# Padding a recurrence's matmuls to the full array, pairing the value products of attention and re-measuring the placing costs, in a hybrid decoder trunk

## The chip, the cores and the metric

The kernel runs on one core of a Trainium2 chip. The metric is the device time of one execution in microseconds (us).

## The reference

One layer with a residual, on x of 512 tokens by 2048 channels, all in float32:

```python
h = _rms(x, norm_g[l])
proj = h @ w_in[l]                       # 57 column tiles of 128
r, k, v, ga, wd, ad = _split(pa, ...)    # 12 RWKV heads of 64, after a token shift
def step(state, inp):
    sa = einsum('bhvk,bhk->bhv', state, -kk_t)
    state = state * w_t + sa[..., None] * (kk_t * a_t) + v_t[..., None] * k_t
    return state, einsum('bhvk,bhk->bhv', state, r_t)
...
z = einsum('bhqd,bhkd->bhqk', q, k)      # 12 stick-breaking attention heads, blocks of 128
w = where(causal, exp(log_sigmoid(z) + after), 0.0)
o = einsum('bhqk,bhkd->bhqd', w, v)
...
y = concatenate([ya, yb, yc], axis=-1) @ w_out[l]
x = x + y
```

Branch B is a trailing mean over 2 to 16 tokens and a small matmul. Each branch is gated by a SiLU of a part of the projection, and the RWKV output goes through a group norm first.

## The kernel before

TensorE (PE) computes the projection one column tile at a time (`project`): 16 blocks of the contraction, and for each the three products of a split into a high and a low part (`three`), so 48 matmuls of 128 x 512 named `pj` a tile, in the rounded type float32r. Six pairs of heads follow each other: four RWKV tiles, four attention tiles each; then eight tiles of the pooling branch. At the end the output projection (`oacc`) takes four column blocks of 512, each 192 matmuls over the 16 branch tiles.

Everything else is written as generators (`rwkv(p)`, `attention(p)`, `pooling(g)`), and `pump` resumes them between the `pj` matmuls. A generator yields a function made by `need` that says from when its next step may be placed. That time comes from `Pace`, a table of costs that counts the PE's matmuls as a clock and books work of VectorE (DVE), ScalarE (ACT) and GpSimd (POOL). So the order of PE's instructions is fixed when the program is built, and each engine executes its own instructions in that order. `high_priority` moves an instruction ahead on its engine.

For a pair of heads, `rwkv(p)` builds decay factors, then per chunk of 64 tokens the coupling matrices (`gm`, L588). The triangular inverse of 32 x 32 blocks is made on DVE, after a trip through DRAM (`s1`, `s2`), in 30 dependent steps of two instructions on `xblk` and `pr` (L620 to 626); two sets of 16 small products (`q1`, `q2`) put the blocks of an inverse together in `lt`. Then eight chunks follow each other serially (L687 to 717): product `w` and its copy `wsb`; product `u` with the inverse and its copies into `uv`; product `s` that updates the state, `se` and `uv`; and two products that add up the output `y`. Every one of these is issued once for each head, on 64 rows or 64 columns of the array. After the last chunk come the group norm (products `mu` and `var`) and the gate. `rwkv(p+1)` starts when `done[("mid", p)]` is set, just before the chunks of pair p.

`attention(p)` computes the scores `z` of a head in four products of 128 rows and four of 64 rows (the correction with `klo`, L778), and the value products `o` of one head at a time on 64 columns (L831). Where a float32 matmul (not float32r) is issued, the trace shows it as two instructions on PE; they are called passes.

All tiles are done before the output projection: `while len(tasks) > 1: pump(True)` (L940), which places what is left without asking `need`.

Of the kernel before, what the change touches and what calls it, by code (L numbers as in the profile page):

```python
# [8 lines left out]
F32 = mybir.dt.float32  # L9
# [43 lines left out]
BANKS = {"pj": 2, "g": 3, "c": 3}  # L53
# [3 lines left out]
EVACUATE = 25  # L57
DL = 4.0
# [28 lines left out]
Y_TILE = {("a", i): i for i in range(6)} | {("b", i): 6 + i for i in range(4)} | {("c", i): 10 + i for i in range(6)}  # L87


class Pace:  # L90
# [37 lines left out]
    def cost(self, eng, f, out, ins):  # L128
        n = self.free(out)
        if eng == "act":  # L130
            return 0.2 + n * 0.00083
        if eng == "pool":
            if f in ("memset", "affine_select"):
                return 0.05 + n * 0.0011
            return 0.08 + n * (0.0028 if f == "tensor_scalar" else 0.0033)
# [16 lines left out]
    def matmul(self, out, lhsT, rhs):  # L152
        n = self.free(rhs)
        m = self.free(lhsT)
        if rhs.dtype == F32R:
            c = max(n / 2400.0, m * 0.00083)
        else:
            c = max(4 * max(n, 64) / 2400.0, 0.1) * (0.6 if m <= 64 or rhs.shape[0] <= 64 else 1.0)
# [45 lines left out]
def hybrid_trunk_kernel(ctx: ExitStack, tc: tile.TileContext, x, xT, w_in, w_out, vecs, consts, up_w, pool_w, out, tap=None):  # L204
# [15 lines left out]
    tp = ctx.enter_context(tc.tile_pool(name="tp", bufs=14))  # L220
# [57 lines left out]

    hh = [hp.tile([P, T], F32R, tag=f"hh{k}", name=f"hh{k}") for k in range(KT)]
# [14 lines left out]
    for pl, tag, parts in ((ap, "q2", 1), (ap, "k2", 1), (ap, "w3", 1), (rp, "bk", 2), (rp, "bkt", 2), (rp, "rx", 2),  # L294
                           (rp, "uv", 2), (rp, "amr", 3), (ap, "wt", 2)):
        xt = pl.tile([P, parts, T], F32, tag=tag, name=name("x"))
# [208 lines left out]

    def rwkv(p):
# [13 lines left out]
        mm(dec, upl[lo, 0:P], wd2[lo, :], False, True)  # L520
# [4 lines left out]
        mm(av, upl[hi, P:2 * P], ad2[hi, :], False, True)  # L525
# [35 lines left out]
        amr = rp.tile([P, NC_, 3, C], F32, tag="amr", name=name("amr"))  # L561
        for h, s in ((0, lo), (1, hi)):
# [7 lines left out]
        dve.tensor_tensor(amr[:, :, 2, :], r3, e[:, :, 1:], ALU.mult)  # L570
# [7 lines left out]
        lt = rp.tile([P, NC_, C], F32, tag="lt", name=name("lt"))  # L578
        ms = strict.rearrange("p (o t) -> p o t", o=1)
        mi = incl.rearrange("p (o t) -> p o t", o=1)  # L580
        for half in range(2):
            cs = slice(4 * half, 4 * half + 4)
            for h, s, other in quad:
                yield need(*([amr, bk] if half == 0 and h == 0 else []), tag="g")
# [6 lines left out]
                dve.tensor_tensor(lt[s, cs, :], g4[s, :, 0, :], ms[s].to_broadcast([HD, 4, C]), ALU.mult)  # L591
# [5 lines left out]
        s2v = s2.rearrange("(c h b) s t -> s c h b t", h=2, b=2)  # L597
        for h in range(2):
            for b in range(2):
                r0 = h * HD + b * B  # L600
                dma(out=s1v[:, :, h, b, :], in_=lt[r0:r0 + B, :, b * B:(b + 1) * B])
# [7 lines left out]


        nblk = rp.tile([P, B, B], F32, tag="bk", name=name("nblk"))
        xblk = tmp("xblk", 8 * B).rearrange("p (i t) -> p i t", t=B)
        s1r = s1.rearrange("k (i g) t -> g k i t", g=4)
        s2r = s2.rearrange("k (i g) t -> g k i t", g=4)
        for r in range(4):
            dma(out=nblk[r * B:(r + 1) * B], in_=s1)
        dma(out=xblk, in_=s1r)
        yield soon(xblk)
        pr = tmp("pr")
        for j in range(1, B - 1):  # L620
            m = B - 1 - j
            ni = (j + 3) // 4
            prv = pr[:, :ni * m].rearrange("p (s t) -> p s t", t=m)
            dve.tensor_tensor(prv, xblk[:, 0:ni, j:j + 1].to_broadcast([P, ni, m]),
# [427 lines left out]
```

## Time and profile before

| | |
|---|---|
| median of 3 runs | 1089.75 us (1088.41 to 1089.97) |
| the profiled execution | 1089.68 us; span from its first to its last instruction 1088.0 us |
| busy: PE, DVE, ACT, POOL | 98%, 68%, 39%, 13% of the span |
| mean granted clock of TensorE | 0.993 |
| first and last `pj`, first and last `oacc` (start) | 42.1 and 907.8, 908.0 and 1083.9 us |

A busy share counts overlapped, pipelined instructions; the distance from the start of one PE instruction to the start of the next is what each costs. An edge, in what follows, is the extra distance where a matmul on the whole array stands next to one on a part of it.

### The profile page before, as it was taken

To read this page: it belongs to the slowest core of one execution; us is meant where nothing else is said; L and a number is where in the kernel's file an instruction comes from. 1 tells how busy PE (TensorE), PEld (TensorE's weight loads), DVE (VectorE), ACT (ScalarE), POOL (GpSimd) and SP (SyncE) were. 2 spreads that over 40 slices of the span, in tenths; PEclk is the share of its full clock that TensorE was granted. 3 is DMA by queue.
4 is the path that set the end of the run, shared out by engine and by line. 5 is a ranking of instruction groups with operands and counts; after the bars stand their busy time and mean duration, and the time that the engine had idled before them with its cause. 6 is when DMAs were issued, how large, how long until landed. Compare 5 with 4: busy or idle time off the path is not lost.

```text
span 1088.0 us, 14731 instructions
## 1 busy us (share of the span) xinstructions
PE 1066.2 (98%) x5552; PEld 801.3 (74%) x5552; DVE 737.6 (68%) x1596; ACT 427.8 (39%) x670; POOL 143.1 (13%) x208
## 2 busy tenths in 40 slices
PE   9998999999999999999999999999999999999998
PEld 7877766687666877668766787667776677888887
DVE  6266978759787797778877799777986457223232
ACT  6453525235353354334543345524443235111111
POOL 0031113101132011210211102210021111000000
PEclk9999999999999999899999999999999999999999
DMA  9513231132211321113221132112221125444232
GB/s 329 204 63 105 80 93 40 56 92 84 84 48 51 107 85 66 58 59 97 86 76 39 64 115 77 61 58 84 100 78 55 48 94 163 149 154 137 96 137 75
DMA packets 58185, 101.92 MB, mean 94 GB/s; under 512 B 29312, under 2 KB 30720, under 8 KB 58112
## 3 DMA queue, kind: packets, MB, share of 16 engines
q1 hardware_dynamic: 58112, 100.96, 28.2%
q8 instruction: 44, 0.72, 0.3%
q14 instruction: 29, 0.24, 0.1%
HBM read 95.17 MB, written 5.77 MB: 93 GB/s over the span
## 4 chain that ended last, share of the span: by engine, by line
PE 80%; DVE 10%; issue 4%; ACT 2%; DMA 2%; POOL 2%; SPq 0%; POOLq 0%; DVEq 0%; ACTq 0%
PE pj L350 45%; PE oacc L350 15%; PE first L350 3%; PE o L350 2%; PE z L350 2%; DVE w L198 2%; DVE wl L198 2%; PE gm L350 2%; PE y L350 2%; PE w L350 2%; PE wT L354 1%; DVE xblk L198 1%; PE u L350 1%; POOL e L198 1%; PE s L350 1%
## 5 line engine op out<-in xcount | busy, mean ns | idle before, releaser
L350 PE MATMUL pj<-hl,wh 128*128 128x512 f32 x864 | 349.0, 404 | 0.0
L350 PE MATMUL pj<-hh,wh 128*128 128x512 f32 x864 | 347.9, 403 | 1.0 <-DVE u L198 0.8
L350 PE MATMUL pj<-hh,wl 128*128 128x512 f32 x864 | 347.6, 402 | 0.0
L198 DVE TENSOR_TENSOR wl<-raw,wh 128x1024 fp32r<-128x1024 f32 x140 | 172.1, 1229 | 168.6 <-ACT wh L198 162.8
L198 ACT CAST wh<-raw 128x1024 fp32r<-128x1024 f32 x140 | 147.0, 1050 | 312.7 <-PE pj L350 187.5
L350 PEld LDWEIGHTS pj<-hh,wh 128*128 128x128 f32 x864 | 163.1, 189 | 38.0 <-issue 4.4
L350 PEld LDWEIGHTS pj<-hh,wl 128*128 128x128 f32 x864 | 163.2, 189 | 35.4 <-issue 0.4
L350 PEld LDWEIGHTS pj<-hl,wh 128*128 128x128 f32 x864 | 163.1, 189 | 35.5 <-issue 1.2
L350 PE MATMUL oacc<-wl,yh 128*128 128x512 f32 x256 | 100.1, 391 | 0.8 <-DVE wl L198 0.8
L350 PE MATMUL oacc<-wh,yl 128*128 128x512 f32 x256 | 99.6, 389 | 0.0
L350 PE MATMUL oacc<-wh,yh 128*128 128x512 f32 x256 | 99.6, 389 | 0.0
L198 POOL TENSOR_SCALAR e<-e 128x512 f32<-128x512 f32 x28 | 49.0, 1749 | 327.9 <-ACT e L198 327.6
L198 POOL TENSOR_TENSOR d<-u 128x512 f32<-128x512 f32 x25 | 34.2, 1370 | 230.9 <-DVE u L198 148.6
L350 PEld LDWEIGHTS oacc<-wl,yh 128*128 128x128 f32 x256 | 48.0, 188 | 11.5 <-DVE wl L198 1.3
L350 PEld LDWEIGHTS oacc<-wh,yl 128*128 128x128 f32 x256 | 48.1, 188 | 10.0 <-issue 0.2
L350 PEld LDWEIGHTS oacc<-wh,yh 128*128 128x128 f32 x256 | 48.0, 188 | 10.0
L198 DVE TENSOR_TENSOR xblk<-xblk,pr 128x60 f32<-128x60 f32 (+8 forms) x180 | 44.5, 247 | 4.1
L198 ACT ACTIVATE e<-e 128x512 f32<-128x512 f32 x50 | 31.4, 629 | 39.1 <-POOL e L198 38.8
L198 DVE TENSOR_TENSOR_SCAN w<-kon,n 128x512 f32<-128x512 f32 (+3 forms) x48 | 39.3, 841 | 6.6 <-POOL n L198 6.5
L198 DVE TENSOR_TENSOR pr<-xblk,nblk 128x60 f32<-128x60 f32 (+8 forms) x180 | 38.7, 215 | 4.4
L198 DVE TENSOR_TENSOR u<-pj,rstd 128x512 f32<-128x512 f32 x50 | 34.3, 686 | 8.3 <-PE pj L350 7.9
L198 ACT ACTIVATE n<-n 128x512 f32<-128x512 f32 (+1 forms) x72 | 38.9, 557 | 1.3
(195 smaller groups left out, 1262.7 us busy)
## 6 DMA issues: line engine op xcount, KB each, us to landing
raw<-in_w_in SPq DMA_DIRECT2D x108, 512.0 KB, 3.4
raw<-in_w_out SPq DMA_DIRECT2D x32, 512.0 KB, 3.4
xs<-in_x SPq DMA_DIRECT2D x8, 512.0 KB, 4.7
xr<-in_x SPq DMA_DIRECT2D x16, 256.0 KB, 5.3
out<-xr SPq DMA_DIRECT2D x16, 256.0 KB, 3.2
fr<-in_w_in SPq DMA_DIRECT2D x12, 256.0 KB, 7.4
nblk<-s SPq DMA_DIRECT2D x24, 128.0 KB, 4.9
x<-in_xT SPq DMA_DIRECT2D x5, 512.0 KB, 7.4
```

The costliest lines, as they stand in the source:

```text
L198: return call(*args, **kw)
L350: pe.matmul(o, lhsT, rhs, start=start, stop=stop)
L354: pe.transpose(o, src, ident)
```

## The change

- **Full-size products.** `amr` and `lt` become lasting buffers whose unused halves are zero, so `w`, `u`, `s`, both `y` products and `gm` are single matmuls on 128 rows and 128 columns for both heads. `w`, `u` and `s` of a chunk share one PSUM bank (`wus`), and `y` of four chunks another. The low-order products of `dec`, `av` and `z` run over all 128 rows; `z` gets a zero-free copy `kl2` of the correction in both halves, made on POOL.
- **Paired value products.** `attention` handles both heads in one pass at the end: for each key block the product of head 0 and that of head 1 are issued one behind the other, on different columns of the array.
- **Placing costs.** `Pace.cost` and `Pace.matmul` get other numbers: a DVE instruction starts at 0.165 us instead of 0.065, a scan counts twice, copies on DVE are no longer halved, a matmul costs a little more.
- **The inverse** is a generator of its own, `inverse(p, s1, s2)`, spawned after `tr`; it yields after every third step instead of every sixth, and `rwkv(p)` waits for `done[("inv", p)]`.
- **Copies ahead.** The DVE copies between the products of a chunk are moved ahead by `SCAN` (40) places. `se` moves from DVE to POOL.
- **The end.** The branch tiles enter the output projection in `Y_ORDER`, with the last pair's (5 and 15) at the end, and nothing waits for all tasks any more: `split_y` places steps with `pump(True)` until the tile that it needs is done.
- The `tp` pool has 13 buffers instead of 14.

```diff
+SCAN = 40
+Y_ORDER = [0, 1, 2, 3, 4, 10, 11, 12, 13, 14, 6, 7, 8, 9, 5, 15]
...
-        if f in ("tensor_scalar", "tensor_copy", "memset") and not any(self.key(a) in self.read_psum for a in ins):
+        if f == "tensor_tensor_scan":
+            n *= 2
+        if f in ("tensor_scalar", "memset"):
             n *= 0.5
-        return 0.065 + n * 0.00104
+        return 0.165 + n * 0.00104
...
-            c = max(n / 2400.0, m * 0.00083)
+            c = max(n / 2400.0 + 0.010, 0.19 * m / 128)
...
+    def inverse(p, s1, s2):
...
+            if j % 3 == 0:
+                yield soon(xblk)
...
+        done[("inv", p)] = True
...
-                    rhs = amr[s, cc, 0:3:2, :] if h == 0 else amr[s, cc, 1:3, :]
-                    mm(g[:, j * P:(j + 1) * P], bk[s, cc, :, :], rhs)
+                    mm(g[:, j * P:(j + 1) * P], bk[:, cc, :, :], amr[:, cc, h:4:2, :])
...
+        spawn(inverse(p, s1, s2))
...
+        while not done.get(("inv", p)):
+            yield None
...
-            for h, s, o in quad:
-                mm(wps[s, 0:C], amr[:, cc, h, :], uv[:, cc, h, :])
+            mm(wps, amr[:, cc, 0:2, :], uv[:, cc, :, :])
             wsb = rp.tile([P, C], F32, tag="wsb", bufs=2, name=name("wsb"))
-            dve.tensor_copy(out=wsb, in_=wps[:, 0:C])
+            with tc.high_priority(offset=SCAN):
+                dve.tensor_copy(out=wsb[lo, :], in_=wps[lo, 0:C])
+                dve.tensor_copy(out=wsb[hi, :], in_=wps[hi, C:P])
...
-                    dve.tensor_scalar(se[s, :], uv[s, cc, h, :], ec[s, cc:cc + 1], None, ALU.mult)
+                    pool.tensor_scalar(se[s, :], uv[s, cc, h, :], ec[s, cc:cc + 1], None, ALU.mult)
...
+            mm(ups, lt[:, cc, :, :], wsb)
...
+            mm(yps, uv[:, cc, :, :], amr[:, cc, 2:4, :], True, False)
...
+                mm(sps, bkt[:, cc, :], uv[:, cc, :, :])
...
-                    mm(z[:, off:off + (i + 1) * P], q2[s, i * P:(i + 1) * P], klo[s, 0:(i + 1) * P], False, True)
+                    mm(z[:, off:off + (i + 1) * P], q2[:, i * P:(i + 1) * P], kl2[:, 0:(i + 1) * P], False, True)
...
-            for j in range(4):
-                mm(o[s, j * P:T], vt[:, j, s], wt[:, pos[j]:pos[j] + T - j * P], j == 0, j == 3)
+            for j in js:
+                for h, s in ((0, lo), (1, hi)):
+                    mm(o[s, j * P:T], vt[:, j, s], parts[h][:, pos[j]], j == 0, j == 2)
...
-    while len(tasks) > 1:
-        pump(True)
...
-        while 6 <= k < 10 and tasks:
+        while not done.get(ready[k]):
             pump(True)
```

The change moves instructions. Three places, as the built programs have them. First PE in the sixth (last) pair's chunks before, inside the projection (`y`, `u`, `s`, `w` are the chunk products, x2 for the two heads; `pj` is the projection):

```order
L350 MATMUL pj_7811<-hh_97,wh_7727 128x512
L350 MATMUL s_7833<-uv_7311,bkt_6720 64x64 x2
L350 MATMUL y_7821<-rx_6721,uv_7311 64x64 x2
L350 MATMUL pj_7811<-hl_113,wh_7727 128x512
L350 MATMUL pj_7811<-hh_97,wl_7728 128x512
L350 MATMUL w_7844<-uv_7311,amr_6710 64x64 x2
L350 MATMUL pj_7811<-hh_98,wh_7727 128x512
L350 MATMUL y_7852<-amr_6710,uv_7311 64x64 x2
L350 MATMUL pj_7811<-hl_114,wh_7727 128x512
L350 MATMUL u_7855<-wsb_7847,lt_6722 64x64 x2
```

Now the fifth pair's chunks on PE, in the output projection, after its first 48 `oacc` matmuls (`wus` with `amr` is w, with `wsb` is u, with `bkt` is s):

```order
L364 MATMUL oacc_7266<-wl_7278,yh_7318 128x512
L364 MATMUL oacc_7266<-wh_7277,yl_7319 128x512
L364 MATMUL wus_7430<-uv_7089,amr 128x128
L364 MATMUL y_7439<-amr,uv_7089 128x128
L364 MATMUL q_1216_7388<-xt_7385,lt 32x32 x16
L364 MATMUL q_1218_7408<-lt,w_1217_7389 32x32 x16
L364 MATMUL wus_7430<-wsb_7432,lt 128x64
L364 MATMUL wus_7430<-uv_7089,bkt_6855 128x128
L364 MATMUL y_7439<-rx_6856,uv_7089 128x128
L364 MATMUL wus_7447<-uv_7089,amr 128x128
L364 MATMUL y_7439<-amr,uv_7089 128x128
```

All eight chunks and the products `mu` and `var` of the fifth pair follow each other there with no other matmul between them; the next `oacc` stands behind `var` and the sixth pair's `dec` and `av`. In the first four pairs the chunk products still stand between `pj` matmuls. The sixth pair's chunks stand in the same way 120 `oacc` matmuls later, with 28 `oacc` of the next column block among its last product, `mu` and `var`. Before, both pairs were through all chunks within the projection.

Third, DVE at the beginning of the sixth pair's chunks now (`wsb` is the copy behind product w, `pr` and `xblk` are the inverse):

```order
L204 COPY uv_7707<-vt_7708 64x4x64 x2
L204 COPY wsb_8031<-wus_8029 64x64 x2
L204 TENSOR_TENSOR wl_8190<-raw_8187,wh_8189 128x1024
L204 TENSOR_TENSOR pr_7914<-xblk_7733,nblk_7732 128x30
L204 MEMSET xblk_7733 32x8
L204 TENSOR_TENSOR xblk_7733<-xblk_7733,pr_7914 128x30
L204 TENSOR_TENSOR pr_7914<-xblk_7733,nblk_7732 128x29
```

The first copy of the chunks now stands ahead of all 60 instructions of the pair's inverse; before, it stood behind them. At the fifth pair it stands ahead of the last 16.

## Rows read from the trace of the kernel before

**Rows 1.** The page, part 1: busy time, share, instructions by engine.
```profile
PE 1066.2 (98%) x5552; PEld 801.3 (74%) x5552; DVE 737.6 (68%) x1596; ACT 427.8 (39%) x670; POOL 143.1 (13%) x208
```

**Rows 2.** Stretch 960 to 1080 us, `oacc`: length, busy (count) by engine, clock.
```profile
960.00:1080.00 120.00, 120.00 (x531) 99.36 (x530) 5.33 (x8) 1.00 0.32 107
```

**Rows 3.** Stretch 485 to 615 us, one pair's period, `pj`, same columns.
```profile
485.00:615.00 130.00, 100.11 (x386) 69.44 (x384) 5.50 (x8) 1.00 0.24 75
```

**Rows 4.** Timeline, 860 to 864 us: start, length, engine, instruction, count.
```profile
860.34 0.34 PE L350 MATMUL s<-uv,bkt 128*64 128x64 f32 x4
...
860.72 0.50 PE L350 MATMUL pj<-hl,wh 128*128 128x512 f32 x1
...
861.05 0.40 PE L350 MATMUL pj<-hh,wl 128*128 128x512 f32 x1
...
861.38 0.35 PE L350 MATMUL w<-uv,amr 128*64 128x64 f32 x4
...
861.66 0.49 PE L350 MATMUL pj<-hh,wh 128*128 128x512 f32 x1
...
861.79 0.23 DVE L198 COPY wsb<-w 128x64 f32<-128x64 f32 x1 [0.44 <-PE w L350]
...
863.17 0.33 PE L350 MATMUL u<-wsb,lt 64*64 64x64 f32 x4
...
863.55 0.48 DVE L198 COPY uv<-u 64x64 f32<-64x64 f32 x2 [1.54 <-PE u L350]
```

**Rows 5.** Waits of PE: us in total, times, longest.
```profile
PE w L350 <- DVE uv L198: 4.2, 5, 1.2
```

**Rows 6.** Timeline of PE, 876 to 879 us.
```profile
876.12 0.40 PE L350 MATMUL var<-sh,bmean_r 128*128 128x512 f32 x1
...
876.59 1.88 PE L350 MATMUL po<-pd,pw 128*128 128x512 f32 x4
...
878.53 0.39 PE L350 MATMUL pj<-hh,wh 128*128 128x512 f32 x1
```

**Rows 7.** Timeline of PE, 129 to 132 us.
```profile
129.00 0.40 PE L350 MATMUL z<-k,q 128*128 128x512 f32 x1
...
131.63 0.50 PE L350 MATMUL pj<-hh,wh 128*128 128x512 f32 x1
```

**Rows 8.** Timeline of PE, 490 to 492 us.
```profile
490.91 1.16 PE L350 MATMUL gm<-amr,bk 64*128 64x128 f32 x8
```

**Rows 9.** Timeline of PE, 329 to 333 us.
```profile
329.98 2.37 PE L350 MATMUL o<-wt,vt 128*64 128x512 f32 x8
...
332.27 0.49 PE L350 MATMUL pj<-hh,wh 128*128 128x512 f32 x1
```

**Rows 10.** The page, part 5: steps of the inverse; busy us, mean ns.
```profile
L198 DVE TENSOR_TENSOR xblk<-xblk,pr 128x60 f32<-128x60 f32 (+8 forms) x180 | 44.5, 247 | 4.1
...
L198 DVE TENSOR_TENSOR pr<-xblk,nblk 128x60 f32<-128x60 f32 (+8 forms) x180 | 38.7, 215 | 4.4
```

**Rows 11.** Timeline of DVE, 147 to 158 us.
```profile
148.19 0.07 DVE L198 MEMSET xblk<- 32x8 f32 x1
...
157.08 0.70 DVE L198 STREAM_TRANSPOSE xt<-lt 128x512 f32<-128x512 f32 x1
```

**Rows 12.** Timeline of DVE, 863 to 882 us.
```profile
865.63 0.69 DVE L198 TENSOR_TENSOR sl<-yc,sh 128x512 fp32r<-128x512 f32 x1 [1.60 <-ACT sh L198]
...
869.96 0.69 DVE L198 TENSOR_TENSOR yc<-yc,mu 128x512 f32<-128x512 f32 x1 [1.35 <-PE mu L350]
...
871.99 0.69 DVE L198 TENSOR_TENSOR sl<-sq,sh 128x512 fp32r<-128x512 f32 x1 [1.35 <-ACT sh L198]
...
879.75 0.69 DVE L198 TENSOR_TENSOR y<-yc,y 128x512 f32<-128x512 f32 x1
```

**Rows 13.** Timeline of ACT, 863 to 880 us.
```profile
876.79 0.69 ACT L198 ACTIVATE sq<-var,biases 128x512 f32<-128x512 f32 x1 [3.49 <-PE var L350]
```

**Rows 14.** Stretch 442.3 to 449 us, PE to POOL, then the granted clock.
```profile
442.30:449.00 6.70, 6.70 (x29) 4.37 (x28) 4.82 (x15) 4.48 (x8) 2.57 (x3) 0.50 0.01 2
```

More of the change, by code (lines that the diff above doesn't have):

```diff
@@ L52 @@
 NFIRST = 3
-BANKS = {"pj": 2, "g": 3, "c": 3}
+BANKS = {"pj": 2, "g": 3, "c": 2, "y": 1}
 MARGIN = 1.5
@@ L504, in hybrid_trunk_kernel @@
     B = 32
+    def inverse(p, s1, s2):
+        nblk = rp.tile([P, B, B], F32, tag="bk", name=name("nblk"))
+        xblk = tmp("xblk", 8 * B).rearrange("p (i t) -> p i t", t=B)
+        s1r = s1.rearrange("k (i g) t -> g k i t", g=4)
+        s2r = s2.rearrange("k (i g) t -> g k i t", g=4)
+        for r in range(4):
+            dma(out=nblk[r * B:(r + 1) * B], in_=s1)
+        dma(out=xblk, in_=s1r)
+        yield soon(xblk)
+        pr = tmp("pr")
+        for j in range(1, B - 1):
+            m = B - 1 - j
+            ni = (j + 3) // 4
+            prv = pr[:, :ni * m].rearrange("p (s t) -> p s t", t=m)
+            dve.tensor_tensor(prv, xblk[:, 0:ni, j:j + 1].to_broadcast([P, ni, m]),
+                              nblk[:, j:j + 1, j + 1:B].to_broadcast([P, ni, m]), ALU.mult)
+            dve.tensor_tensor(xblk[:, 0:ni, j + 1:B], xblk[:, 0:ni, j + 1:B], prv, ALU.add)
+            if j % 3 == 0:
+                yield soon(xblk)
+        for r in range(4):
+            dve.memset(xblk.rearrange("p i t -> p (i t)")[r * B:(r + 1) * B, r:8 * B:B + 4], 1.0)
+        dma(out=s2r, in_=xblk)
+        s2v = s2.rearrange("(c h b) s t -> s c h b t", h=2, b=2)
+        for h in range(2):
+            for b in range(2):
+                r0 = h * HD + b * B
+                dma(out=lt[r0:r0 + B, :, h, b * B:(b + 1) * B], in_=s2v[:, :, h, b, :])
+        done[("inv", p)] = True
     def rwkv(p):
@@ L560, in rwkv @@
         bk = rp.tile([P, NC_, 2, C], F32, tag="bk", name=name("bk"))
-        amr = rp.tile([P, NC_, 3, C], F32, tag="amr", name=name("amr"))
-        for h, s in ((0, lo), (1, hi)):
+        for h, s, other in quad:
+            pool.memset(amr[other, :, h, :], 0.0)
             dve.scalar_tensor_tensor(bk[s, :, h, :], ba3[s], -1.0, ei3[s], ALU.mult, ALU.mult)
@@ new lines, in rwkv @@
+            yield need(uv, margin=TIGHT + 0.1)
+            if not last:
+                mm(sps, bkt[:, cc, :], uv[:, cc, :, :])
+                with tc.high_priority(offset=SCAN):
+                    for h, s, o in quad:
+                        dve.scalar_tensor_tensor(uv[s, cc + 1, h, :], sps[s, h * C:(h + 1) * C], ec[s, cc:cc + 1], se[s, :], ALU.mult, ALU.add)
+            mm(yps, uv[:, cc, :, :], rx[:, cc, :, :], False, True)
+            if cc % 4 == 3:
+                y4 = ybank.rearrange("p (c h t) -> p c h t", c=4, h=2)
+                yo = y[:, (cc - 3) * C:(cc + 1) * C].rearrange("p (c t) -> p c t", t=C)
+                for h, s, o in quad:
+                    act.copy(out=yo[s], in_=y4[s, :, h, :])
@@ L900, in finish @@
             got[(kind, i)] = u
-    first = [cb("first") for _ in range(NFIRST)]
+    first = [bank(("c", "c", "y")[n], "first") for n in range(NFIRST)]
     for kq in range(KT // KQ):
@@ L921, in hybrid_trunk_kernel @@
         row_sums()
+    for h, s, other in quad:
+        pool.memset(amr[other, :, 2 + h, :], 0.0)
+        pool.memset(lt[s, :, 1 - h, :], 0.0)
     def begin():
@@ L936, in hybrid_trunk_kernel @@
         finish(n, project(n))
-    order = list(range(6)) + list(range(10, 16)) + list(range(6, 10))
-    while len(tasks) > 1:
-        pump(True)
     yh, yl = {}, {}
+    ready = {n: ({"a": "gn", "b": "pool", "c": "att"}[br], i) for (br, i), n in Y_TILE.items()}
     def split_y(i):
-        k = order[i]
-        while 6 <= k < 10 and tasks:
+        k = Y_ORDER[i]
+        while not done.get(ready[k]):
             pump(True)
@@ L993, in _pack @@
     w_in = w_in.reshape(len(TILES), P, KT * P)
-    order = list(range(6)) + list(range(10, 16)) + list(range(6, 10))
-    wo = f["w_out"][0].reshape(KT, P, 4, 512)[order]
+    wo = f["w_out"][0].reshape(KT, P, 4, 512)[Y_ORDER]
     w_out = np.ascontiguousarray(wo.reshape(KT // 2, 2, P, 4, 512).transpose(3, 0, 2, 1, 4)).reshape(4, KT // 2, P, 1024)
```

158 lines of the change are left out of this document (68 added, 90 removed).

## The prediction

> **What bounds the kernel.** I read the shares first: PE is busy for 1066 of 1088 us [rows 1], so only work taken off PE, or a wait put on it, moves the time. Next, what of PE's time cannot change. In the output projection a full-size float32r matmul costs 120 / 531 = 0.226 us, call it 0.227 [rows 2]. One pair's period is 130 us with 386 `pj` [rows 3]: 386 x 0.227 = 87.6 us are projection, the other 42.4 us are the small products of RWKV and attention and what they cost at their borders. Then the timeline of one chunk [rows 4] for those borders: the `pj` at 861.05 is followed by w only 0.33 us later, 0.10 more than it costs among its like, though nothing was waited for. I charge 0.10 on the way into a group on part of the array and 0.10 on the way out. This is an edge, and it is what full-size products can save.
>
> The rest of PE's time is not waits: 1088.0 - 1066.2 = 21.8 us idle in all, and the chunk's own wait, w for `uv`, makes 4.2 us of it [rows 5].
>
> **Full-size products.** Do they lose their edges? Rows of a full-size float32 product between `pj` say yes: from `po` to the second `pj` after it, 876.59 to 878.53, there are four passes of 512 columns and one `pj`; (1.94 - 0.23) / 4 = 0.428 us a pass leaves no room for edges [rows 6]. A quarter of it, 128 columns, is 0.107; eight passes of `gm` in 1.16 us with their edges bound it too [rows 8]. I take 0.112.
> - Recurrence. Now s with y takes 860.34 to 860.72 = 0.38 us, with edges 0.58; w takes 861.38 to 861.66 = 0.28, with edges 0.48; I price the first y and u like w [rows 4]. That is 0.58 + 3 x 0.48 = 2.02 us a chunk. After: five products of two passes, 10 x 0.112 = 1.12. Over 48 chunks -43 us; where y and u stand together one pair of edges is already saved, so I take **-42**, bounds -25 (together everywhere) and -44.
> - z: 2.63 us to the next `pj` [rows 7], with the edge behind it 2.73 a head. After: twice 0.227 + 0.170 + 0.114 + 0.112 (512, 384, 256 and 128 columns, by rows 2 and 8) = 1.25. Twelve heads: **-18**.
> - gm: 1.16 us [rows 8] to 8 x 0.112 = 0.90, 24 groups: **-6** (0 to -9). The low products of `dec` and `av` lose an edge each, 12 x 0.2 = 2.4: **-3**.
>
> **Paired value products.** One head's o takes 2.29 us to the next `pj` [rows 9], with an edge 2.49, a pair 5.0. Its stream is 1280 columns in two passes: 2560 / 512 x 0.428 = 2.14. If the two heads, on different columns, run side by side, the pair costs 2.14 + 3 groups x 0.3 of edges = 3.0; if not, 4.28 + 0.9 = 5.2. I take the first, because w's four passes, two a head, take 0.28 us [rows 4] where four full ones in a row would take 0.43: **-12** over six pairs, bounds -12 and +1.
>
> Sum of these: -81 us (-45 to -86 with all bounds at one end). Chunk steps also stand further apart in the first four pairs, which shortens PE's waits: **-8**, between 0 and -14 of the 21.8 idle.
>
> **What the new placing does at the end.** Here the cover goes. Before, all chunks stood among `pj`, and the latency of a chunk was hidden. Now those of the fifth pair stand behind 48 `oacc` and those of the sixth 120 later, each with nothing between. The reason is the order of branch tiles: 12 matmuls a tile, the fifth in `Y_ORDER` is tile 4 (48 = 4 x 12), the fifteenth tile 5 (168 = 14 x 12), and the next `oacc` needs the tile, so PE sits through the pair's remaining chain. DVE's order makes it worse: the copy `wsb` of the first chunk, which needs PE's w, is queued ahead of the pair's inverse steps, 16 instructions in one pair and all 60 in the other, so these too wait until PE gets there. The links, in series:
> - w, 0.4 [rows 4], and the split `wl` queued behind the copy, twice the elements of a 0.69 us operation [rows 12]: 1.3.
> - Inverse steps at 0.247 + 0.215 = 0.46 [rows 10]: 8 of them 3.7, 30 of them 13.9.
> - The trip through DRAM from `memset` to `xt`: 8.8 [rows 11].
> - `xt` 0.70 [rows 11], then q1, copy, q2, copy. Product to end of copies is 0.86 for u [rows 4]; sixteen products instead of two may double it: 2 x 1.6. Together 3.9, an estimate.
> - A chunk: s to w 1.04, w to the end of `wsb` 0.64, u to the end of its copies 0.86, with the semaphores between 2.65, and 0.25 for the second `wsb` copy [rows 4]: 2.9. Eight, less the first w and the last s, 21.2. The move of `se` to POOL has a whole w-to-s leg to hide in.
> - Group norm: last y to the end of `sl` 2.9, an estimate: the copy of y, its two splits and the way to PE, about 0.7 each like those on DVE [rows 12]; `var` at 876.12 to Ln at 876.79 is 0.7 and `mu` is the same again [rows 6, 13]; `yc` to the end of `sl`, 869.96 to 872.68, 2.7 [rows 12]; Ln to the end of y at 880.44, 3.65 [rows 12, 13]; the rounding 0.7: 11.4.
>
> First tail 50.7, second 60.9 us. PE works in each 8 x 1.12 + 4 x 0.428 (`mu`, `var`) = 10.6, which the sum above already holds: 40.1 and 50.3 remain. In the second, 28 `oacc` of the next block fill 6.4, and the wait for the sixth pair's `gm` may add 2 (0 to 4): 45.9. Together **+86**, with q and copies 78 to 95. [...]
>
> [...]
>
> Sum: 1088.0 - 81 - 8 + 86 + 8 = 1093; the profiled execution's time is 1.7 above its span (1089.7), which the median equals. Forecast **1095 us**.
>
> **Rivals.**
> 1. Faster. All 42.4 us a pair beyond `pj` hold more edges than I priced (transposes, `ss`, `tr`), and waits give 14: savings 102. Tails by their lower bound, 78 + 4: 1089.7 - 102 + 82 = 1070; with savings alone at my figure and tails low, 1083. It decides where savings exceed about 95 us. Against it: small groups I did not list stay as they are. For it: every link of the tails is an estimate from covered work, and links may overlap. Chance 0.27.
> 2. o does not run side by side, +13: 1108. For it: float32 passes of o alone take as long as their stream [rows 9], so PE might be limited elsewhere. Chance 0.12.
> 3. Padding costs instead of saving, because today's half-size products of two heads overlap. From rows 4, w's four passes take 0.28 us, 0.07 each; without edges a chunk would have cost 0.28 x 3 + 0.38 = 1.22 against 1.12, so recurrence gives only 5 instead of 42: 1132. Against it the 0.33 us between `pj` and w [rows 4]. Chance 0.04. [...]
> 4. The change does not do what it says: edges come from going between float32r and float32, not from the part of the array. Then some 300 full-size groups still pay 0.2 us: 60 us of the savings vanish, 1155. Rows 6 contradict it. Chance 0.03.
>
> **Chances.** My forecast 0.54, the rivals as above. A measurement of this kernel can tell 0.2%, some 2.2 us, from no change. The forecast's own spread (savings 70 to 86, waits 0 to 14, tails with clock 82 to 106, not all at one end) runs from 1078 to 1115, so some of its low end falls within 0.2% of 1089.75 or below: faster 0.28, same 0.11, slower 0.61. The range 1075 to 1115 leaves out the extremes of rival 1 and rivals 3 and 4.
>
> **What would show it.** In the profile after: distance from a chunk product to the `pj` behind it near 0.22 with no 0.33 before it; z of a head in 1.25; sixteen passes of o in about 3 us; two stretches in the output projection, one tile-4 and one tile-5, in which PE idles some 40 and 46 us beyond its work, chunks there 2.9 apart, and a granted clock below 1. Wrong it would be if the chains stand there with short waits, since DVE had run ahead, or if `pj` next to full-size chunk products still take 0.33.

## The result: 1151 us, and the profile after

| | before | after |
|---|---|---|
| median of 4 runs each | 1089.86 us | 1151.35 us (1147.05 to 1154.09) |
| ratio | | 1.0555, interval 1.0509 to 1.0601 |
| span of the profiled execution | 1088.0 us | 1152.3 us |

Slower was right, the size was not: 1095 us was forecast, and the range ended at 1115. The page of the kernel after, its busy times and two rows of the 40 slices (PE in tenths, and the granted clock in tenths):

```profile
PE 1037.1 (90%) x5084; PEld 832.1 (72%) x5084; DVE 741.7 (64%) x1554; ACT 427.2 (37%) x652; POOL 240.9 (21%) x338
...
PE   9989999989998999999999999899927772789998
...
PEclk9999999999999999999999999899965795589999
```

PE's busy time fell from 1066.2 [rows 1] to 1037.1 us, and the span grew by 64. The two holes in these rows are the two tails. The same by stretches (columns: stretch, length, busy and count of PE, PEld, DVE, ACT, POOL, then granted clock, DMA share, GB/s):

```profile
42.00:825.00 783.00, 748.00 (x3796) 601.30 (x3795) 586.75 (x1192) 344.64 (x537) 210.37 (x288) 0.99 0.25 81
...
840.00:900.00 60.00, 28.85 (x142) 20.80 (x142) 23.92 (x89) 3.67 (x9) 6.64 (x16) 0.52 0.09 24
...
945.00:1015.00 70.00, 34.70 (x166) 26.11 (x166) 30.72 (x121) 4.78 (x10) 5.31 (x12) 0.57 0.14 42
```

The projection ends at 825 us instead of 908, in part because two pairs' chunks are no longer in it. In the tails PE is busy for half of the time or less and has a granted clock of 0.52 and 0.57; from 846 to 904 us and from 950 to 1005 it is 0.50. What PE waited for in the whole run (us in total, times, longest):

```profile
PE q L364 <- DVE xt L204: 42.3, 4, 23.8
PE wus L364 <- DVE uv L204: 20.8, 34, 3.0
PE vps L368 <- DVE w L204: 5.0, 3, 3.9
```

The first tail on PE's timeline (start, length, engine, instruction; in brackets the idle time ahead of it and what ended it):

```profile
838.81 0.38 PE L364 MATMUL wus<-uv,amr 128*128 128x128 f32 x2
...
856.57 0.31 PE L364 MATMUL q<-xt,lt 32*32 32x32 f32 x2 [17.16 <-DVE xt L204]
...
869.97 0.69 PE L364 MATMUL wus<-wsb,lt 128*128 128x64 f32 x2
871.29 0.80 PE L364 MATMUL wus<-uv,bkt 128*128 128x128 f32 x2 [0.64 <-DVE uv L204]
...
872.87 0.77 PE L364 MATMUL wus<-uv,amr 128*128 128x128 f32 x2 [0.35 <-DVE uv L204]
...
874.19 0.69 PE L364 MATMUL wus<-wsb,lt 128*128 128x64 f32 x2
...
904.88 0.63 PE L364 MATMUL oacc<-wh,yh 128*128 128x512 f32 x1
```

From the first w at 838.81 to the next `oacc` at 904.88 are 66.1 us; the prediction had 50.7. A chunk, u at 869.97 to u at 874.19, takes 4.22 us; the prediction had 2.9. The second tail begins at 943.42, and its first `oacc` matmul comes 58.4 us later.

The full-size products did what was claimed. A head's z, now eight full-size matmuls between two `pj`, and a chunk in the projection:

```profile
129.28 0.39 PE L364 MATMUL z<-k,q 128*128 128x512 f32 x1
...
130.55 0.39 PE L364 MATMUL pj<-hh,wl 128*128 128x512 f32 x1
...
562.18 0.39 PE L364 MATMUL pj<-hh,wh 128*128 128x512 f32 x1
562.41 0.38 PE L364 MATMUL wus<-uv,amr 128*128 128x128 f32 x2
562.54 0.48 PE L364 MATMUL pj<-hl,wh 128*128 128x512 f32 x1
562.86 0.40 PE L364 MATMUL pj<-hh,wl 128*128 128x512 f32 x1
```

z takes 1.27 us (129.28 to 130.55) against 2.63 [rows 7]; 1.25 was forecast. The `pj` ahead of w costs 0.23, where it cost 0.33 [rows 4]. The `pj` behind w still costs 0.32.

**Where the time went.** For the table I added up, over all PE matmuls, the distance from the start of one to the start of the next, less idle time ahead of the next, by product; idle time apart. Before: 1065.8 us of work and 17.0 idle. After, outside the two tails: 980.1 and 42.4, the tails themselves 66.1 + 58.4 = 124.5, in which PE has about 20 us of work of its own by the prediction's prices (an estimate). Of the 980.1, 9.0 us are `oacc` matmuls at the lower clock, 0.70 from 904 to 909 us, 0.76 from 918 to 925 and 0.66 from 1012 to 1022 (183.6 us against 174.6 before).

| part | forecast | measured |
|---|---|---|
| PE's own work | -81 | 980.1 + 20 - 9.0 - 1065.8 = -75 |
| PE's waits outside the tails | -8 | 42.4 - 17.0 = +25 |
| the two tails beyond PE's work | +86 | 124.5 - 20 = +105 |
| lower clock around the tails | +8 | +9 |
| together | +5 | +64 (span +64) |

So the work on PE was priced well. Two steps failed: the waits, by 33 us, and the tails, by 19 us.

### The profile page after: what moved, and what is told of

Same layout as the page of the kernel before. It is cut to its first block, busy times and chain, and to the rows that moved or that the text cites. A ratio compares the mean times of both kernels' runs of the same rounds, so it can differ in the third digit from the quotient of the medians.

```text
span 1152.3 us, 13972 instructions
## 1 busy us (share of the span) xinstructions
PE 1037.1 (90%) x5084; PEld 832.1 (72%) x5084; DVE 741.7 (64%) x1554; ACT 427.2 (37%) x652; POOL 240.9 (21%) x338
## 4 chain that ended last, share of the span: by engine, by line
PE 51%; DVE 19%; issue 13%; POOL 6%; ACT 6%; DMA 4%; SPq 0%; POOLq 0%; DVEq 0%; ACTq 0%
PE pj L364 24%; PE oacc L364 14%; PE wus L364 4%; DVE wl L204 4%; POOL e L204 3%; DVE pr L204 2%; DVE xblk L204 2%; DVE w L204 2%; DVE uv L204 2%; ACT e L204 2%; PE gm L364 2%; ACT wh L204 2%; DMA xs<-in_x 1%; PE first L364 1%; PE y L364 1%
## 5 line engine op out<-in xcount | busy, mean ns | idle before, releaser
L364 PE MATMUL pj<-hl,wh 128*128 128x512 f32 x864 | 345.3, 400 | 0.0
L204 DVE TENSOR_TENSOR wl<-raw,wh 128x1024 fp32r<-128x1024 f32 x140 | 179.5, 1282 | 131.8 <-ACT wh L204 130.9
L364 PE MATMUL oacc<-wh,yh 128*128 128x512 f32 x256 | 103.2, 406 | 3.0 <-ACT wh L204 1.1
L204 POOL TENSOR_SCALAR se<-uv,ec 64x64 f32<-64x64 f32 x84 | 52.9, 629 | 210.0 <-DVE uv L204 205.4
L204 POOL CAST kl<-klo 64x512 fp32r<-64x512 f32 x24 | 20.7, 861 | 164.7 <-DVE klo L204 149.7
L204 ACT COPY yc<-y 64x256 f32<-64x256 f32 x24 | 8.8, 367 | 119.0 <-PE y L364 118.7
L204 DVE TENSOR_TENSOR pr<-xblk,nblk 128x60 f32<-128x60 f32 (+8 forms) x180 | 44.0, 244 | 10.7 <-DMA xblk<-s 5.7
L204 DVE TENSOR_TENSOR xblk<-xblk,pr 128x60 f32<-128x60 f32 (+8 forms) x180 | 41.2, 229 | 5.0
```

The costliest lines, as they stand in the source:

```text
L204: return call(*args, **kw)
L364: pe.matmul(o, lhsT, rhs, start=start, stop=stop)
```

## The experiments

Each run stands against runs of the kernel before on the same chip. Their medians were 1092 to 1094 us, against 1089.86 in the result above, so what is compared from one experiment to another is the ratios.

**1. What makes the tails: one cost of the planner.** The changed kernel with one number put back (shown), and with all costs put back (those of POOL, which the change altered too, and of the matmul included):

```diff
-        return 0.165 + n * 0.00104
+        return 0.065 + n * 0.00104
```

> The changed kernel with one number of the placing costs put back: a DVE instruction starts at 0.065 us instead of 0.165. Theory 'placing': this number alone pushes the RWKV chain into the output projection. In this order all chunks of all six pairs stand among pj again, so the two serial tails (105.7 us beyond PE's own work, and 8.4 us of oacc at the lower clock) go, and the savings of PE work stay: 1040 us if the 25 us of additional waits inside the projection stay, 1013 us if they go too. Rival 'structure': the inverse as a task of its own, the copies ahead and the missing drain make the time, whatever the costs: over 1090 us, with PE waits over 60 us in the projection.

> The changed kernel with all placing costs as before (DVE, POOL, matmul). Theory 'the start cost decides': within 8 us of the run with that one number put back. Rival 'the other new costs are worth something': 10 us or more slower than that run, by more PE waits in the projection.

Measured: 1083.70 us, ratio 0.991 (0.9885 to 0.9934), and 1078.25 us, ratio 0.9868 (0.9836 to 0.99). With that one number the chunks of all pairs stand in the projection again, PE's order has no chain alone in the output projection, and both tails are gone: by the two ratios the run is 6% faster than the changed kernel. This is shown: the start cost of 0.165 makes the tails. But neither 1040 nor 1013 came. PE's waits with the start cost put back:

```profile
PE vps L368 <- DVE w L204: 28.3, 6, 5.6
PE wus L364 <- DVE wsb L204: 5.5, 8, 1.4
```

PE's work is 1016.9 us, 49 below the kernel before, and PE idles 60.8 us, 44 more. That the work fell by 49 and not by 75 lies mostly with `pj`, which takes 641 us here and 620 in the changed kernel; the mean granted clock is 0.978 where the kernel before has 0.993. From the first w of a pair to that of the next it is 130 us from the third pair on, the same as before; a stretch of that length (columns as above):

```profile
534.00:664.00 130.00, 121.46 (x642) 96.33 (x642) 102.73 (x233) 55.67 (x90) 37.72 (x51) 0.97 0.23 75
```

So the high cost, which makes the tails, also kept these waits short (25 us more than before instead of 44), and in this order nearly all of the saved work is not collected.

**2. The copies ahead.** The prediction charged the inverse's wait for PE to the copies that `SCAN` moves ahead on DVE.

```diff
-            with tc.high_priority(offset=SCAN):
+            with tc.high_priority(offset=0):
```

> The changed kernel with the copies of the chunks not moved ahead on DVE (offset 0 instead of 40). What the prediction said of the tails: the inverse of the sixth pair waits as a whole for the wsb copy ahead of it, so up to 15 us go: 1137 us. Rival, from the trace after: the inverse's input lands only at about 940.3 and its first step runs at 945.8, so no more than 5 us hang on the copy there, nothing at the fifth pair, and inside the projection the copies now stand behind other DVE work: 1145 to 1160 us.

Measured: 1147.65 us, ratio 1.0501 (1.0471 to 1.053), and the two intervals overlap. Of the 15 us nothing came: from the first w to the next `oacc` the tails are 66.07 and 58.35 us long, where the changed kernel has 66.08 and 58.43. The copies are not what makes the tails long. DVE at the second tail in the changed kernel shows why:

```profile
943.84 0.46 DVE L204 COPY wsb<-wus 64x64 f32<-64x64 f32 x2 [2.69 <-PE wus L364]
...
945.84 0.18 DVE L204 TENSOR_TENSOR pr<-xblk,nblk 128x30 f32<-128x30 f32 x1
```

DVE stood idle for only 2.69 us in front of the copy, and the first step of the inverse follows 2 us behind it; the inverse is late there because the whole chain of the sixth pair is.

**3. The clock in the tails.** 128 x 512 matmuls into an unread bank fill PE's gaps among the chunk products of the tails (the edit in part). If the granted clock of 0.50 is what makes the chunks there long, later chunks should take 2.9 to 3.2 us, though PE has more to do, and the run 1125 to 1138 us; that was the theory.

```diff
+    def busy(o, n):
+        for _ in range(n):
+            pe.matmul(o, hh[15][:, 0:P], hh[15], start=True, stop=True)
...
             mm(yps, uv[:, cc, :, :], amr[:, cc, 2:4, :], True, False)
+            if late:
+                busy(fill, 5)
...
             mm(yps, uv[:, cc, :, :], rx[:, cc, :, :], False, True)
+            if late and not last:
+                busy(fill, 3)
```

> The changed kernel with 128x512 matmuls into an unread PSUM bank put among the chunk products of the two tails (40 or so a pair, two or three in each gap), nothing left out. [...] Rival 'latency': 4.2 us is the latency of copies, semaphores and the y products ahead, the clock plays no part: chunk period 4.2 or longer by the filling, 1150 us or more.

Measured: 1140.39 us, ratio 1.0429 (1.0403 to 1.0455), by the two ratios 1.2% faster than the changed kernel with more work on PE. A chunk now, u to u:

```profile
869.36 0.43 PE L364 MATMUL wus<-wsb,lt 128*128 128x64 f32 x2
869.61 0.94 PE L555 MATMUL fill<-hh 128*128 128x512 f32 x3
870.43 0.49 PE L364 MATMUL wus<-uv,bkt 128*128 128x128 f32 x2
...
872.72 0.43 PE L364 MATMUL wus<-wsb,lt 128*128 128x64 f32 x2
```

3.36 us, and in the chunks of the first tail the granted clock is 0.97 where the changed kernel has 0.50:

```profile
864.00:880.00 16.00, 16.00 (x85) 11.63 (x85) 6.53 (x28) 0.73 (x2) 4.36 (x10) 0.97 0.00 1
```

```profile
864.00:880.00 16.00, 11.72 (x38) 8.85 (x38) 5.57 (x24) 0.73 (x2) 3.54 (x8) 0.50 0.00 0
```

(the filled kernel first, then the changed one). So the clock plays a part, against the rival: with the fillers PE is busy for all of the 16 us and not for 11.72, the granted clock is 0.97 and not 0.50, and a chunk is 0.86 us shorter, of the 1.3 that the prediction missed. What makes the rest isn't shown; the two or three fillers in each gap may take up part of it. The first chunk of each tail gets longer by the fillers, 5.84 and 6.05 us, and the six behind it take 3.24 to 3.41; in the first tail a filler costs 0.46 us in the first chunk (five in 2.28 from 860.62) and 0.28 in a later one (three in 0.83 from 872.96). The total of 1125 to 1138 was missed by 2 us, less than the 4 us between the medians of the kernel before in the two series of runs.

**4. What takes the place of the saved work.** All of the following start from the kernel of experiment 1 with one number put back (ratio 0.991), and ask which wait holds it. First single links: `vps` placed later; `se` and the second half of `amr` on DVE again (the edit of `se` is shown); a larger margin; margin (2.5) and `vps` together.

```diff
-                yield need(vs, tag="g", margin=MARGIN + 2.0)
+                yield need(vs, *blocks.values(), tag="g", margin=MARGIN + 2.0)
```

```diff
-                    pool.tensor_scalar(se[s, :], uv[s, cc, h, :], ec[s, cc:cc + 1], None, ALU.mult)
+                    dve.tensor_scalar(se[s, :], uv[s, cc, h, :], ec[s, cc:cc + 1], None, ALU.mult)
```

```diff
-MARGIN = 1.5
+MARGIN = 3.0
```

> The version with the start cost put back (1083.7 us), and in attention the transposes vps placed only when the planner has the w of the three z blocks of head 0 done, whose banks vps needs. There PE waited 28.3 us for DVE's w in front of vps, six times 4.3 to 5.6. Theory 'a bank asked for too early gives the savings back': these 28 us go, the granted clock rises again with them, nothing replaces them: 1050 to 1060 us. Rival 'DVE, ACT and POOL set the period of 130 us a pair': the wait appears elsewhere on PE with the same sum, and the time stays within 1078 to 1088.

> The version with the start cost put back (1083.7 us), with se and the second half of amr on DVE again instead of POOL. Rival 'POOL': the work moved to POOL (20 to 38 us busy a pair) stands in front of the selects that DVE's scans wait for, so PE's waits fall by 15 us or more: below 1070. Theory 'placing': POOL is not what PE waits for in the end; within 5 us of 1083.7, the vps wait stays near 28.

> The version with the start cost put back (1083.7 us) with MARGIN 3.0 instead of 1.5: every step outside the chunks is placed 1.5 us later, the chunks keep TIGHT. The chain takes up to 407 pj a pair in the order, so the sixth pair's group norm ends just inside the projection. Theory 'placed too early': six vps waits shrink by 1.5 each and others as much: 1060 to 1072. Rival 'period': within 5 us of 1083.7.

> MARGIN 2.5 and the later vps together on the version with the start cost put back. Theory 'placed too early': the waits of PE in the projection fall from 61 to 20 us and the clock returns to 0.99: 1030 to 1045 us, below both kernels. Rival 'period': 1075 or more.

Measured: 1088.68 us, ratio 0.9967 (0.9951 to 0.9983); 1089.32, 0.9965 (0.9947 to 0.9982); 1086.78, 0.9948 (0.9926 to 0.9969); 1091.62, 1.000 (0.9984 to 1.0016). None is faster than 0.991. The later `vps` did what it should and PE's wait for w was gone, but another of the same size stood in its place:

```profile
PE q L364 <- DVE xt L204: 29.7, 7, 5.2
```

So I read a wait as the place where PE, whose order runs ahead, is stopped once a pair, and not as the cause. That is argued: in each of these runs the planner made a new order, so they change more than one link. For the same reason the second run does not clear POOL's `se` and `amr`; it shows only that moving them back did not help.

**5. The inverse.** Moved ahead by 40 places on DVE, without and with all old costs; half of it left out.

```diff
+            with tc.high_priority(offset=40):
                 dve.tensor_tensor(prv, ...)
                 dve.tensor_tensor(xblk[:, 0:ni, j + 1:B], ...)
```

```diff
-        for j in range(1, B - 1):
+        for j in range(1, B // 2):
```

> The version with the start cost put back (1083.7 us), with the 60 steps of the inverse moved ahead by 40 places on DVE; no work added or left out. In that version the inverse takes 28 us a pair, though its steps alone take 15, since other DVE work stands between; and every pair, from the first w to the next pair's first w, takes 130 us, as in the kernel before. Theory 'RWKV loop': the serial chain gm, DRAM trip, inverse, DRAM trip, chunks, gm of the next pair sets those 130 us; it gets 10 us a pair shorter and the time falls: 1035 to 1060. Rival 'DVE's throughput' (103 of 130 us busy a pair): the other DVE work waits instead, 1078 to 1090.

> The version with all placing costs as before (1078.3 us), with the inverse's steps moved ahead by 40 places on DVE. Theory 'RWKV loop': 1030 to 1055, below both kernels. Rival 'DVE's throughput': within 6 us of 1078.

> The version with the start cost put back (1083.7 us), with the second half of the inverse's steps (16 to 30) left out. That takes 30 DVE instructions of about 0.2 us and some 12 us of chain a pair. Theory 'RWKV loop' and rival 'DVE's throughput' both expect less: 1030 to 1060. Rival 'PE's clock and edges': PE stays the bound, within 5 us of 1083.7.

Measured: 1077.52 us, ratio 0.9856 (0.9837 to 0.9875); 1078.40, 0.9856 (0.9828 to 0.9884); 1096.43, 1.0043 (1.0026 to 1.006). The first gains 0.5% only, and the second nothing clear of noise (0.9868 without). The first did not test its theory: in the last three pairs the inverse still takes 27.3 us from the first to the last step (27.5 without). Leaving out half made the kernel slower, against every theory, because the planner knew of it: it placed q and the chunks so much earlier that PE waited for `xt` again, 22.3 us. In experiments 6, 8 and 9 the planner books what it booked before, and only what an engine executes is changed.

**6. The order nearly kept.** Half of the inverse left out on DVE but still booked in the planner (some 4% of PE's instructions still stand elsewhere in the trace):

```diff
+            if j >= B // 2:
+                pace.record("dve", "tensor_tensor", prv, [xblk, nblk])
+                pace.record("dve", "tensor_tensor", xblk[:, 0:ni, j + 1:B], [xblk, prv])
+            else:
```

> The version with the start cost put back (1083.7 us), with the second half of the inverse's steps left out on DVE, but still booked in the planner, so that the order on PE is the same as in that version (unlike the run that left them out of both). Theory 'DVE and the chain behind it run later than the planner's clock': with 6 us less of DVE work a pair and the same order, each wait of PE (vps for w 28 us, wus for wsb 5.5, lt 3.1) gets shorter: 1050 to 1070. Rival 'PE waits for ACT and POOL in front of DVE': the vps wait stays at 24 to 28 us, 1076 to 1084.

Measured: 1063.16 us, ratio 0.972 (0.9701 to 0.9739), 1.9% less than with the whole inverse, some 20 us. The wait in front of `vps` fell from 28.3 to 17.0, and the mean granted clock rose from 0.978 to 0.988:

```profile
PE vps L368 <- DVE w L204: 17.0, 6, 3.6
```

This takes away DVE work and makes the serial chain shorter, both. The run that was to tell them apart takes 0.6 us out of each weight split (the edit in part; PE then reads the half that is made twice):

```diff
-        dve.tensor_tensor(wl, raw, wh.bitcast(F32), ALU.subtract)
+        pace.record("dve", "tensor_tensor", wl, [raw, wh])
+        nc.vector.tensor_tensor(wl[:, 0:512], raw[:, 0:512], wh[:, 0:512].bitcast(F32), ALU.subtract)
...
```

> The version with the start cost put back (1083.7 us), with the low parts wl of the weights made on DVE for half the columns only and used twice, booked in the planner as before, so that PE's order stays the same. It takes 0.6 us from each of 18 weight splits a pair, some 10 us of DVE work, and nothing from the chain of the inverse and the chunks. Theory 'DVE's work as a whole makes it late': as much as with the half booked inverse (6 us less a pair gave 20 us) or more: 1045 to 1066. Rival 'RWKV chain': what the half inverse gave was its shorter chain (inverse 27 us to 13.5 us); work off the chain gives under 8 us: 1076 to 1084.

Measured: 1078.54 us, ratio 0.9867 (0.9829 to 0.9905), 0.4% less, some 5 us, which is within the intervals of both. DVE's busy time fell from 733 to 657 us, by far more than with the half inverse (695), and the wait in front of `vps` stayed at 27.9 us:

```profile
PE vps L368 <- DVE w L204: 27.9, 6, 6.0
```

and its page, busy times:

```profile
PE 1016.0 (94%) x5084; PEld 810.3 (75%) x5084; DVE 656.7 (61%) x1554; ACT 429.0 (40%) x652; POOL 220.7 (20%) x338
```

The time falls on the side of the rival, "RWKV chain", but the run does not settle it. The weight splits stand between the steps of the inverse, which got shorter too: 25.2 us from its first to its last step, for 27.5. And DVE's own order changed: `xt` now stands in front of n and w, which PE's `vps` waits for, and waits itself for the inverse to come back from DRAM, 5.11 and 1.98 us:

```profile
524.29 0.43 DVE L204 STREAM_TRANSPOSE xt<-lt 32x256 f32<-32x256 f32 x1 [5.11 <-DMA lt<-s]
...
525.21 0.69 DVE L204 SCALAR_TENSOR_TENSOR n<-z,n 128x512 f32<-128x512 f32 x1
...
527.88 0.43 DVE L204 STREAM_TRANSPOSE xt<-lt 32x256 f32<-32x256 f32 x1 [1.98 <-DMA lt<-s]
528.35 1.22 DVE L204 TENSOR_TENSOR_SCAN w<-kon,n 128x512 f32<-128x512 f32 x1
```

In the kernel of experiment 1 the same wait has another origin. There `xt` waits for nothing at this place. The scaled projection tile `u`, from which ACT and POOL make a sigmoid (e), stands on DVE behind the last step of the inverse, and on ACT the n of attention stands behind that sigmoid:

```profile
520.75 0.39 PE L364 MATMUL pj<-hh,wl 128*128 128x512 f32 x1
...
523.16 0.17 DVE L204 TENSOR_TENSOR xblk<-xblk,pr 128x8 f32<-128x8 f32 x1
...
523.49 0.69 DVE L204 TENSOR_TENSOR u<-pj,rstd 128x512 f32<-128x512 f32 x1
...
524.21 0.63 ACT L204 ACTIVATE e<-u 128x512 f32<-128x512 f32 x1 [1.88 <-DVE u L204]
...
525.01 1.90 POOL L204 TENSOR_SCALAR e<-e 128x512 f32<-128x512 f32 x1 [4.74 <-ACT e L204]
...
526.95 1.30 ACT L204 ACTIVATE e<-e 128x512 f32<-128x512 f32 x2 [2.10 <-POOL e L204]
...
528.15 0.58 ACT L204 ACTIVATE n<-z 128x512 f32<-128x512 f32 x1
...
530.43 0.69 DVE L204 SCALAR_TENSOR_TENSOR n<-z,n 128x512 f32<-128x512 f32 x1 [4.11 <-ACT n L204]
...
534.05 1.11 PE L368 MATMUL vps<-kon,u 128*128 128x128 f32 x4 [4.36 <-DVE w L204]
```

PE ends the tile with the `pj` at 520.75, so at 521.14; DVE comes to `u` 2.34 us later, and from there to `vps` it is 10.56 us, while PE is ready for `vps` 8.55 us behind the tile. The difference is the wait. With half of the inverse left out, DVE is free when the tile is done:

```profile
508.24 0.69 DVE L204 TENSOR_TENSOR u<-pj,rstd 128x512 f32<-128x512 f32 x1 [2.45 <-PE pj L364]
...
519.13 0.83 PE L368 MATMUL vps<-kon,u 128*128 128x128 f32 x4 [2.60 <-DVE w L204]
```

`u` is 0.04 us late here, from `u` to `vps` it is 10.89 us, and 2.60 us of the wait are left. The third to the sixth pair are alike in both runs (`u` 2.3 to 2.7 us late against 0.04). So the half inverse made this wait shorter because it no longer stands in front of `u` on DVE, and not by a shorter way through DRAM. In the weight-split run `u` is 0.2 us late as well, and `xt` took its place.

**7. Both late links mended, and the weight splits later.**

```diff
-AHEAD = 300
+AHEAD = 100
```

> The version with the start cost put back, with both the later vps and the inverse ahead. With the later vps alone PE waited 29.7 us for the inverse (q for xt), with the inverse ahead alone 26.1 us for w in front of vps. Theory 'two single late links': with both mended the waits fall from 61 to 20 us: 1030 to 1050. Rival 'the whole order is ahead of the chip': another link is late by the same amount: 1070 to 1085.

> The same with MARGIN 2.5. Theory 'two single late links': 1025 to 1045. Rival 'the whole order is ahead of the chip': a margin moves each step by a constant and wins nothing in a period, 1075 to 1092, as with the margin and the later vps (1091.6).

> The version with the start cost put back and the inverse ahead (1077.5 us), with the weight splits moved ahead by 100 places instead of 300. DVE sits idle 151.6 us, 51 times, in front of wl for ACT's wh, which itself waits for PE to give a weight buffer back; what is queued behind wl on DVE waits with it. Theory 'wl in front holds DVE': 1045 to 1065. Rival: those are times at which DVE has nothing else ready: within 5 us, or slower where pj then waits for wl.

Measured: 1082.24 us, ratio 0.9901 (0.9883 to 0.992); 1090.55, 0.9975 (0.9958 to 0.9993); 1075.90, 0.985 (0.9815 to 0.9884). The first two fall on the side of "the whole order is ahead of the chip": q waited 26.9 us for `xt`. The third (0.985) is the same as without it (0.9856), as its rival said.

**8. Was there room in the kernel before?** There, the 64-row products of z left out on PE and booked as before (the edit in part; some 11% of PE's instructions stand elsewhere in the trace):

```diff
-                    mm(z[:, off:off + (i + 1) * P], q2[s, i * P:(i + 1) * P], klo[s, 0:(i + 1) * P], False, True)
+                    pace.matmul(z[:, off:off + (i + 1) * P], q2[s, i * P:(i + 1) * P], klo[s, 0:(i + 1) * P])
```

> The kernel before, with the low-order products of z (64 rows, four a head) left out on PE but still booked in the planner, so that the order stays nearly the same. A head's z group takes 2.63 us there; the four full products alone 0.62; 12 heads, 24 us less work on PE. The prediction's first sentence, only work taken off PE moves the time: 24 us faster than the kernel before. Rival 'the other engines need the same 130 us a pair': PE waits in their place, under 10 us faster.

Measured: 1079.70 us, ratio 0.9884 (0.9852 to 0.9915), 12 us of 24. z's work fell by 23.7 us. PE's waits gave 5 us of it back, and its other products 7, the chunk products 4 of them, which now stood apart oftener. The truth lies between the two expectations: of PE's work taken away in the kernel before, about half arrived.

**9. POOL's copies.** In the kernel of experiment 1, steps of the inverse on DVE are long while POOL copies `kl` (start, length):

```profile
517.62 2.66 POOL L204 CAST kl<-klo 64x512 fp32r<-64x512 f32 x2 [39.43 <-DVE klo L204]
...
519.70 0.63 DVE L204 TENSOR_TENSOR pr<-xblk,nblk 128x42 f32<-128x42 f32 x1
520.36 0.20 DVE L204 TENSOR_TENSOR xblk<-xblk,pr 128x42 f32<-128x42 f32 x1
```

The copies on ACT, booked as before:

```diff
-            pool.tensor_copy(out=kl2[s, :], in_=klo[s, :])
-            pool.tensor_copy(out=kl2[other, :], in_=klo[s, :])
+            for d in (s, other):
+                pace.record("pool", "tensor_copy", kl2[d, :], [klo[s, :]])
+                nc.scalar.copy(out=kl2[d, :], in_=klo[s, :])
```

> The version with the start cost put back (1083.7 us, ratio 0.991 to the kernel before), with the 24 copies of the correction kl2 made on ACT instead of POOL, booked in the planner as before, so that the order on PE stays. On POOL they take 20.7 us in the changed kernel, and steps of the inverse beside them take 0.63 us instead of 0.20. Theory 'POOL holds DVE': the inverse gets 2 us a pair shorter and the RWKV chain with it: ratio 0.980 to 0.987. Rival 'ACT's queue is as bad a place', or the stretched steps cost nothing: ratio 0.988 to 0.996.

Measured: 1074.54 us, ratio 0.9827 (0.9803 to 0.985), 0.8% less than with the copies on POOL, some 9 us: the price that the theory gave. PE's order is the same to the last instruction. The inverse got shorter by 0.8 to 2.4 us a pair (26.6 for 27.5 in the last three), and the wait in front of `vps` fell by 7 us:

```profile
PE vps L368 <- DVE w L204: 21.1, 6, 4.0
```

The traces show the way. From the third pair on DVE comes to `u` 1.5 us behind its tile instead of 2.3 to 2.7, and PE's waits are 3.4 to 4.0 us instead of 4.4 to 4.7. POOL also executes the selects between n and w, but in these pairs they waited for DVE's n in both runs, not for a copy. This is the fastest version here that computes everything, 1.7% faster than the kernel before and, by the two ratios, 6.9% faster than the changed one.

## Why the prediction was wrong

- **What bounds the kernel.** "Only work taken off PE, or a wait put on it, moves the time" was the first step to fail. 98% busy says that PE had no idle time; it does not say how close behind the other engines are. In this kernel, whose order is fixed for five engines, PE's saving arrives only as far as the chains through DVE, ACT, POOL and DRAM get ready earlier too. In experiment 8 half of it arrived in the kernel before; in experiment 1, with the tails and the high cost removed, 49 us less work met 44 us more of waits.
- **PE's work.** Right: -75 for -81. z 1.27 us (1.25 forecast). A chunk's edges: gone on the way in, but a full-size float32 group keeps about 0.09 on the way out, the 0.32 us behind w. I had read none at all from [rows 6]. Over the whole projection the median `pj` in front of a chunk group costs 0.33 us before and 0.23 after, behind one 0.34 and 0.31, and 0.227 among its like. Summed over the trace, the chunk products fell from 67.3 us for 48 chunks to 32.1 for the 32 outside the tails, and `pj`, which holds most of the edges, by 22.6 us; z fell by 16.1; o by 11.3 (12 forecast), so the two heads do run side by side, and rival 2 falls.
- **Waits.** "Chunk steps also stand further apart ... which shortens PE's waits: -8" was wrong: +25, of which some 21 us in the projection and the rest beside the tails. The step costed what the order does to the chunks and left out that PE now arrives earlier everywhere else. That this is the cause is shown in the order of experiment 1 (`u` behind the inverse, experiment 6); in the changed kernel itself no run took these waits apart.
- **The tails.** Their place was right. The reason that the prediction gives, the order of the branch tiles, tells only behind how many `oacc` they stand; that the chunks leave the projection at all comes from the start cost of 0.165 (experiment 1), which it did not weigh. Of the links, two were mis-sized. The chunk was priced with the legs that it has at a granted clock of 1.00 (860 to 864 us in the kernel before), 2.9 us; at 0.50 it takes 4.22. From u to u, the seven steps take 29.3 us in the first tail and 30.1 in the second, against 20.3 forecast: 18.8 us, the size of the whole miss of the tails (q with its copies, 5.1 and 5.0 us instead of 3.2, is made up for by other links). No run shows the +8 that the sum has for the clock. What the runs showed in its place: 9.0 us more for the `oacc` behind the tails, and 18 more for the 14 chunk steps at a clock of 0.50 (14 x 1.3), of which experiment 3 took back 0.8 or more a step behind the first chunk. (In the kernel before, the clock is 0.50 over the 6.7 us of [rows 14]; PE was idle for 1.16 us ahead of the w at 440.63.) On the other side, the inverse of the fifth pair hardly waited for PE, against "DVE's order makes it worse": DVE reached the copy at 844.3, and the steps behind it were done at 849.4. That order plays no part that can be measured (experiment 2).
- **The rivals.** None was the right one. Rival 1 had a price for larger savings but none for savings that do not arrive. Rival 3 falls with the chunk products (67.3 us for 48, 32.1 for 32) and z. Rival 4 falls on the way in, where the edge is gone; on the way out 0.09 us is left behind each float32 group, about half of its price of 0.2.

**Open.** What arrives of work left out is shown for half of the inverse with the order nearly kept (20 us), and for POOL's copies with the order kept (9 us). Of the 61 us of PE's idle time in the kernel of experiment 1, 28 stand in front of `vps`, with the origin shown in experiment 6. What the rest hangs on, link by link, and why even with `u` in time `vps` waits 2.6 us a pair, is not settled: each link that was mended alone or in twos was followed by another of like size. An order made anew from measured end times of every engine wasn't tried.

## What to carry to other kernels

A busy share of 98% tells which engine ends last, not how much it may shrink: before costing a saving, take the same work away with the order kept, and see what arrives. When a planner's cost is raised to make waits shorter, count the serial chains in its time: here 0.1 us more for each DVE instruction turned a period of 384 `pj` for the longest chain into 565 to 587, and the chain fell out of its cover. Where a chain loses its cover, do not price its links from covered work: here a chunk took 4.22 us at a granted clock of 0.50, and 2.9 was forecast from work at 1.00.

## What the runs showed of the hardware

Steps of the inverse on DVE can be long while POOL works: 0.63 us beside POOL's copy, 0.20 for the same shape right after the copy ended at 520.28 (experiment 9). In the kernel before, a step of 16 elements at 529.23 took 1.26 us beside POOL's y (1.29 us), where the one ahead of it took 0.18. There, 14 of the 48 steps that overlap POOL's work took over 0.3 us, and in the changed kernel 17 of 46; of the 312 and 314 others none did. The change raised POOL's busy time by 98 us (143 to 241), and the prediction weighed none of it against DVE.

The second is an edge behind a full-size float32 group, 0.09 us on the first float32r matmul (0.32 against 0.23), with both on the whole array. What differs there is the type and the number of columns; the two were not tried apart.
